# One pair of PSUM banks for two spreadings, and quarter loads of the last down group's weights into staging tiles

## The chip, the cores and the metric

The kernel runs on one core of a Trainium2 chip. The metric is the device time of one execution in microseconds (us). Engines are called PE (TensorE matmul), PEld (its weight loads), DVE (VectorE), ACT (ScalarE), POOL (GpSimd) and SP (SyncE, which issues nearly all DMAs here).

## The reference

One layer of a streaming encoder, for 1024 prompt tokens and 64 sample tokens together (T = 1088 columns), model width 1024, all in float32: a mixer (retention and sliding-window attention), cross attention, and a SwiGLU feed-forward, each with a residual add, then a final RMS norm. The change touches the feed-forward and what leads into it:

```python
def rms_norm(x, g=None):
    y = xf * lax.rsqrt(jnp.mean(xf * xf, axis=-1, keepdims=True) + EPS)
    ...
def swiglu(x, g_ffn, w_gate, w_up, w_down):
    hn = rms_norm(x, g_ffn)
    return (jax.nn.silu(hn @ w_gate) * (hn @ w_up)) @ w_down
...
hp = hp + swiglu(hp, g_ffn[l], w_gate[l], w_up[l], w_down[l])
y_prompt = rms_norm(hp, g_final)
```

D_FF is 2816, that is 22 blocks of 128 rows.

## The kernel before, in words

Activations lie transposed: 128 partitions of features, 1088 columns of tokens, split into two halves of 544 columns, each worked in two pieces of 272. Every float32 operand is split into a rounded high part (a cast on ACT, L123) and the rest (a subtraction on DVE, L124), and a product is three matmuls: high by high, high by low, low by high (L205, L206 and L208 in the feed-forward, L149 to L151 elsewhere).

**The products of the feed-forward** are Strassen's (Winograd's form): weights and operands are taken as 2 by 2 blocks, and seven products P1 to P7 replace eight. `strassen` (L247) runs them in the order P1 (operand B11), P2 (B21), P6 (T2), P5 (T1), P7 (T3), P3 (B22), P4 (T4); DVE and POOL add up the sums u1, u2, u5, u3. The weights' side is made by `weight_ops` (L166) from two raw tiles of two halves each (a11, a12; a21, a22): POOL forms a11-a21 for P7 (L183), a21+a22 for P5 (L184), a22-a11 for P6 (L186) and a12-that for P3 (L189), in place, and every result is cast and subtracted into a tile `wq`. So P6 comes after a chain: cast and subtraction of a11 (P1), L183, cast and subtraction (P7), L186, cast (P6).

**Spreading.** A norm factor per token is found with tokens on partitions (`some_rstd`) and is spread to all partitions by three 128x128 matmuls with the identity into a PSUM tile (`spread`, L323, matmuls L330) and a copy on ACT (L331). The 1088 columns go in chunks of 384, 384 and 320. After cross attention the first chunk is spread at once; the other two are put in `self.later` (L1263) and run inside the first, plain gate product (`plain`, L225): three of its four sums are open, each in a pair of banks, when `run_later` spreads chunk 1 and chunk 2. The PSUM pool has four pairs of banks ("pst", L1331). What follows them on PE is the fourth sum, beginning with operand B12 (tile `b12`).

**Down projection** (`down`, L1443). The 22 blocks are taken in groups of 8, 8 and 6. In each group the eight 128-row strips of the output go in four pairs, m = 0, 2, 4, 6, called here pair 1 to pair 4. The sums stay in tiles y: y[0] is `rstd_f`, the others show as y0, y1, y2. DVE adds a product to y (L1453), POOL adds a sum u (L1455). In the last group (n = 384 columns per block) P2 and P4 are left out of Strassen's seven and are computed by a tail (`finish`, products L149 with weights `wb`), so a pair has five products: P1, P6, P5, P7, P3. When the second half of a strip is complete, `complete` (L1459) squares it on ACT (L1463 for the first, L1466 into a tile `sq` for the others) and DVE adds the square to `rstd` (L1467). After pair 3 ACT loads the table for the square root and takes a dummy root (L1504).

The weights of a pair are loaded into two raw tiles (pool of two buffers), each 128x768 in the last group, by SP (L117). The operands of the next group are loaded back from memory (`fetch`, L1435) into **staging tiles** named `hl` and are then cast and subtracted into the operand tiles. The staging tiles rotate over two pools: "hl" with 4 buffers (L1330) and "hl2" with 6 (L1408), two tiles from "hl", then three from "hl2":

```python
self.pools = (self.hl, self.hl, more, more, more) * 2   # set once, L1409
self.pools = self.pools[1:] + self.pools[:1]            # per tile, in fetch
...
sq = self.hl.tile([P, HALF], F32, tag="hl", name="sq")  # complete
```

Which of the two a tile falls on is set by how many were taken before it. The `sq` tiles of `complete` come from pool "hl" too. In the last group B21 and T4 are fetched after pair 1's products are written down.

**What sets the order.** Each engine runs its own queue in order. A scheduler with a model of the times decides the order of the instructions on each engine when the kernel is built, SP's loads among them; a tile that takes over a buffer makes its first writer wait for the last user of the tile before it. So an edit can move instructions of lines that it doesn't touch.

Of the kernel before, what the change touches and what calls it, by code (L numbers as in the profile page):

```python
# [11 lines left out]
F32 = mybir.dt.float32  # L12
# [7 lines left out]
P = 128  # L20
# [20 lines left out]
HALF = T // 2  # L41
# [68 lines left out]
class Kernel:  # L110
# [54 lines left out]

    def weight_ops(self, raws, n=512, skip=()):  # L166

        nc = self.nc
        half = [[raws[i][:, j * n:(j + 1) * n] for j in range(2)] for i in range(2)]
        (a11, a12), (a21, a22) = half  # L170
        add, sub = ALU.add, ALU.subtract
        w = {}

        def put(name, src):
            if name in skip:
                return
            q = w[name] = self.new_op()
            self.split(src, q[:, 0, :n], q[:, 1, :n])

        tt = nc.gpsimd.tensor_tensor  # L180
        put("P1", a11)
        put("P2", a12)
        tt(out=a11, in0=a11, in1=a21, op=sub)  # L183
        tt(out=a21, in0=a21, in1=a22, op=add)  # L184
        put("P7", a11)
        tt(out=a11, in0=a22, in1=a11, op=sub)  # L186
        put("P6", a11)
        put("P5", a21)
        tt(out=a12, in0=a12, in1=a11, op=sub)  # L189
        put("P3", a12)  # L190
        put("P4", a22)
        return w
# [127 lines left out]

        return [(min(a, n - P), P) for a in range(0, n, P)]

    def spread(self, out, r):  # L323

        nc = self.nc
        n = out.shape[1]
        spans = self.spans(n)
        pb = self.norm_psum("pb")
        for i, (a, w) in enumerate(spans):
            nc.tensor.matmul(pb[:, a:a + w], r[:, i:i + 1].broadcast_to([P, P]), self.ident, start=True, stop=True)  # L330
        nc.scalar.copy(out, pb[:, :n])  # L331
# [898 lines left out]
    def cross_out_phase(self):  # L1230
        nc, tc, io = self.nc, self.tc, self.io
        with ExitStack() as ctx:
            cq = ctx.enter_context(tc.tile_pool(name="cq", bufs=1, reuse_waits="tile"))
            ctx.enter_context(self.plain_psum(side="right"))
            pn = ctx.enter_context(tc.tile_pool(name="pnc", bufs=1, reuse_waits="tile", space=PSUM, side="right"))
            self.norm_psum = lambda name: pn.tile([P, 512], F32, tag="n", name=name)
            xg = self.ring_tiles(0, KT // 2, "xg", F32)
            self.xg = [xg[k // 2][:, k % 2, :] for k in range(KT)]
            self.ops, self.slots = {}, {}
            units = [lambda m=m: self.unit(io["w_co"][m], KT) for m in range(KT)]  # L1240
            norms, rs = [], []
            for m, u, (c0, n) in self.m_major(units, CH, tail=2):
                if m == 4 and not self.ops:
                    self.operands_early()
                    self.first_sums()
                x = cq.tile([P, 384], F32, tag="hx", bufs=4, name="hx")[:, :n]
                self.load(x, self.d_h[0][m, :, c0:c0 + n])
                ps = self.dense(u, self.couts, c0, n)
                nc.vector.tensor_tensor(out=x, in0=ps, in1=x, op=ALU.add)
                self.store(self.d_h[1][m, :, c0:c0 + n], x)  # L1250
                acc = self.rstd_f[:, c0:c0 + n]
                nc.vector.scalar_tensor_tensor(self.xg[m][:, c0:c0 + n], x, self.gains[:, 2, m:m + 1],
                                               self.rstd[:, c0:c0 + n], ALU.mult, ALU.mult)
                self.add_square(acc, x, m == 0, cq, n)
                if m == KT - 1:
                    root = self.root[:, c0 // 384, :]
                    def first(acc=acc, root=root):
                        rs.append(self.some_rstd(acc, times=root))

                    norms.append((first, lambda acc=acc, i=len(norms): self.spread(acc, rs[i])))  # L1260
                    if len(norms) < 3:
                        self.later += norms[-1][:3 - len(norms)]
            self.later, self.last_roots = [norms[1][1], norms[2][1]], norms[2][0]  # L1263

    def op_tiles(self, ring, names):
        for a in range(0, len(names), 2):
# [168 lines left out]
    def fetch(self, name, group):  # L1435
        n0 = sum(GROUPS[:group]) // 2
        for k in range(GROUPS[group] // 2):
            self.pools = self.pools[1:] + self.pools[:1]
            a = self.pools[0].tile([P, HALF], F32, tag="hl", name="hl")
            self.load(a, self.d_op[OPS.index(name), n0 + k])  # L1440
            yield a

    def down(self, starts):  # L1443
        nc, io = self.nc, self.io
# [4 lines left out]
        half = lambda m, t: y[m][:, t * HALF:(t + 1) * HALF]  # L1449
        def add(m, i, t, ps, sb):  # L1450
            v = half(m + i, t).rearrange("p (b c) -> p b c", b=2)
            if ps is not None:
                nc.vector.tensor_tensor(out=v, in0=ps, in1=v, op=ALU.add)  # L1453
            if sb is not None:
                nc.gpsimd.tensor_tensor(out=v, in0=sb, in1=v, op=ALU.add)  # L1455
# [3 lines left out]
        def complete(m, c0, n):  # L1459
            acc, o = self.rstd[:, c0:c0 + n], y[m][:, c0:c0 + n]  # L1460
            if c0 not in begun:
                begun.add(c0)
                nc.scalar.activation(acc, o, AF.Square)  # L1463
            else:
                sq = self.hl.tile([P, HALF], F32, tag="hl", name="sq")[:, :n]
                nc.scalar.activation(sq, o, AF.Square)  # L1466
                nc.vector.tensor_tensor(out=acc, in0=acc, in1=sq, op=ALU.add)  # L1467

        def load_half(tile, m, a, b):
            self.load(tile.rearrange("p (k m) -> p k m", m=P), io["w_down"][m, :, a:b, :])  # L1470

        for gi, g in enumerate(GROUPS):
            last = gi == len(GROUPS) - 1
            f0, n = starts[gi], g * P // 2
            for m in range(0, KT, 2):
                def emit(i, t, ps, sb, m=m):
                    add(m, i, t, ps, sb)
                    if last and t == 1:
                        complete(m + i, HALF, HALF)

                raws = [self.wp.tile([P, 1024], F32, tag="raw", bufs=2, name="raw") for i in range(2)]
                for i in range(2):
                    load_half(raws[i][:, :2 * n], m + i, f0, f0 + g)
                if m == KT - 4 and not last:
                    for name in ("B11", "B21" if gi == 0 else "T2"):
                        self.ahead[name, gi + 1] = list(self.fetch(name, gi + 1))
                if gi == 0:
                    for i in range(2):
                        self.load(y[m + i], self.d_h[1][m + i])
                if m == 0 and not last:  # L1490
                    self.plain(self.plain_weights(raws, n), self.ops, emit)
                    for name in ("T2", "T1", "T3", "T4"):
                        self.load_operand(name, gi)
                else:
                    w = self.weight_ops(raws, n, ("P2", "P4") if last else ())
                    if m == KT - 2 and not last:
                        self.refill = lambda name, gi=gi: self.turn(name, 1) if gi == 0 else self.turn_last(name)
                    self.strassen(w, self.ops, emit, last)
                    self.refill = None
                    if m == 0:  # L1500
                        for name in ("B21", "T4"):
                            self.load_operand(name, gi)
                if last and m == KT - 4:
                    nc.scalar.activation(self.root[:, 0, :1], self.rstd[:, HALF:HALF + 1], AF.Sqrt)  # L1504
        rest = []
        for m in range(0, KT, 2):
            raw = self.wp.tile([P, 1024], F32, tag="raw", bufs=2, name="raw")
# [189 lines left out]
```

## Time and profile before

| | |
|---|---|
| three runs | 2239.42, 2241.54, 2242.42 us (median 2241.54) |
| profiled execution | 2239.58 us, span 2237.8 us from first to last instruction |
| mean granted PE clock | 0.986 |
| last down group, pair 1's first matmul | 2141.53 us |
| tail's first matmul | 2194.96 us |
| DMA over the span | 290.86 MB, mean 130 GB/s |

Times in the rows are us from the start of the span, then the duration. In a row of the timeline the square brackets give the idle time of the engine before it and what ended it. A row of stretches gives the busy time of each engine, with the count of its instructions, then PE's granted clock (1.00 is full), the DMA share and GB/s. At full clock matmuls with 272 columns follow each other every 0.125 us, while a row shows some 0.29 us for one, as they overlap. The tail of the span, from about 2219 us on, is a chain of norm steps and stores that neither part of the change touches.

### The profile page before, as it was taken

The numbers are of one execution on the slowest core, as the hardware profiler recorded it, in microseconds if no ns is written. First come the engines' busy times: TensorE is split into PE (matmuls) and PEld (weight loads), VectorE is DVE, ScalarE is ACT, GpSimd is POOL, SyncE is SP. The second block draws the span as 40 slices with busy tenths as digits, with TensorE's granted clock in tenths as the row PEclk, the third lists the DMA queues.
The fourth block names the chain that finished last, engine by engine and source line by source line (L and its number), as shares of the span: only waits on it lengthen the run. The fifth ranks groups of instructions, "written<-read, shape, count | busy, mean of one in ns | idle before, by whom it ended". The sixth has DMA issues, their size and how long they took to land.

```text
span 2237.8 us, 41757 instructions
## 1 busy us (share of the span) xinstructions
PE 2171.3 (97%) x16434; PEld 2106.8 (94%) x16434; DVE 1600.4 (72%) x2655; ACT 884.7 (40%) x1897; POOL 690.5 (31%) x466
## 2 busy tenths in 40 slices
PE   9999999999999989999999999999999999999996
PEld 9899999999999977779999998999999999999986
DVE  8986878676687668876455555668777777778588
ACT  7333333435444355553133333333222222334243
POOL 1441533342253112220000000014555555434462
PEclk9999999999999999999999999999999999999998
DMA  5433345443445475326443112422332332475233
GB/s 205 156 111 110 117 123 137 133 127 113 167 152 178 151 229 169 114 75 208 130 154 107 55 48 65 134 85 88 122 130 101 102 122 89 142 273 182 84 102 109
DMA packets 182599, 290.86 MB, mean 130 GB/s; under 512 B 40290, under 2 KB 110850, under 8 KB 182402
## 3 DMA queue, kind: packets, MB, share of 16 engines
q1 hardware_dynamic: 177794, 279.26, 39.3%
q10 hardware_dynamic: 4608, 8.91, 1.1%
q8 instruction: 130, 2.13, 0.4%
q14 instruction: 67, 0.55, 0.1%
HBM read 196.95 MB, written 91.16 MB: 129 GB/s over the span
## 4 chain that ended last, share of the span: by engine, by line
PE 75%; DVE 7%; DMA 4%; issue 1%; ACT 1%; POOL 1%; SPq 0%; DVEq 0%; ACTq 0%; POOLq 0%
PE pq L208 14%; PE pq L206 14%; PE pq L205 14%; PE pd L149 7%; PE pd L151 7%; PE pd L150 7%; PE pout L1000 1%; DMA hl<-d_op 1%; PE pp L984 1%; DVE wq L124 1%; PE pss L942 1%; DMA ld<-d_swa 1%; DVE B L124 1%; DMA raw<-w_ret_out 1%; PE pk L699 0%
## 5 line engine op out<-in xcount | busy, mean ns | idle before, releaser
L124 DVE TENSOR_TENSOR wq<-raw,wq 128x512 fp32r<-128x512 f32 (+1 forms) x505 | 450.1, 895 | 124.8 <-ACT wq L123 122.6
L123 ACT CAST wq<-raw 128x512 fp32r<-128x512 f32 (+1 forms) x505 | 307.6, 614 | 569.9 <-PE pq L208 262.7
L205 PE MATMUL pq<-T,wq 128*128 128x272 f32 x1832 | 493.9, 289 | 6.2 <-DVE u L252 3.6
L206 PE MATMUL pq<-T,wq 128*128 128x272 f32 x1832 | 493.9, 289 | 0.0
L206 PE MATMUL pq<-B,wq 128*128 128x272 f32 x1592 | 429.3, 289 | 8.4 <-DVE B L124 8.4
L205 PE MATMUL pq<-B,wq 128*128 128x272 f32 x1592 | 426.7, 288 | 0.0
L208 PE MATMUL pq<-T,wq 128*128 128x272 f32 x1832 | 384.4, 290 | 3.4 <-DVE wq L124 3.4
L183 POOL TENSOR_TENSOR raw<-raw 128x512 f32<-128x512 f32 (+1 forms) x59 | 79.4, 1345 | 894.8 <-DVE rs_r L291 483.8
L205 PEld LDWEIGHTS pq<-T,wq 128*128 128x128 f32 x1832 | 346.7, 189 | 7.1 <-DVE u L252 3.7
L206 PEld LDWEIGHTS pq<-T,wq 128*128 128x128 f32 x1832 | 346.8, 189 | 0.3 <-issue 0.3
L208 PE MATMUL pq<-B,wq 128*128 128x272 f32 x1592 | 334.0, 290 | 0.0
L206 PEld LDWEIGHTS pq<-B,wq 128*128 128x128 f32 x1592 | 300.7, 189 | 10.3 <-DVE B L124 10.0
L205 PEld LDWEIGHTS pq<-B,wq 128*128 128x128 f32 x1592 | 300.1, 189 | 0.7 <-issue 0.4
L208 PEld LDWEIGHTS pq<-T,wq 128*128 128x128 f32 x1832 | 292.0, 191 | 4.6 <-DVE wq L124 3.8
L208 PEld LDWEIGHTS pq<-B,wq 128*128 128x128 f32 x1592 | 253.5, 190 | 0.5 <-issue 0.3
L252 DVE TENSOR_TENSOR u<-pq,u 128x544 f32<-128x544 f32 x177 | 127.5, 720 | 111.7 <-PE pq L208 111.1
L186 POOL TENSOR_TENSOR raw<-raw 128x512 f32<-128x512 f32 (+1 forms) x59 | 85.3, 1446 | 125.2 <-DVE wq L124 122.6
L970 POOL TENSOR_TENSOR t<-t,den 128x768 f32<-128x768 f32 (+2 forms) x34 | 47.8, 1406 | 167.7 <-DVE den L968 49.9
L571 DVE TENSOR_TENSOR stage<-pq,u 128x544 f32<-128x544 f32 x112 | 80.3, 717 | 26.6 <-PE pq L208 25.8
L184 POOL TENSOR_TENSOR raw<-raw 128x512 f32<-128x512 f32 (+1 forms) x59 | 89.2, 1512 | 3.7
L1455 POOL TENSOR_TENSOR y<-u,y 128x544 f32<-128x544 f32 x38 | 62.6, 1658 | 72.4 <-DVE y L1453 54.4
L189 POOL TENSOR_TENSOR raw<-raw 128x512 f32<-128x512 f32 (+1 forms) x59 | 83.2, 1411 | 4.4
(373 smaller groups left out, 4674.2 us busy)
## 6 DMA issues: line engine op xcount, KB each, us to landing
hl<-d_op SPq DMA_DIRECT2D x85, 272.0 KB, 4.4
d_qkv<-stage SPq DMA_DIRECT2D x44, 272.0 KB, 2.3
d_op<-stage SPq DMA_DIRECT2D x44, 272.0 KB, 2.1
d_op<-ht SPq DMA_DIRECT2D x44, 272.0 KB, 3.3
raw<-w_gate SPq DMA_DIRECT2D x22, 512.0 KB, 3.5
raw<-w_up SPq DMA_DIRECT2D x22, 512.0 KB, 3.6
d_gate<-stage ACTq DMA_DIRECT2D x32, 272.0 KB, 2.8
raw<-w_down SPq DMA_DIRECT2D x16, 512.0 KB, 4.4
```

The costliest lines, as they stand in the source:

```text
L123: self.last_cast = self.nc.scalar.copy(hi, src).ins
L124: return self.nc.vector.tensor_tensor(out=lo, in0=src, in1=hi.bitcast(F32), op=ALU.subtract).ins
L149: mm(ps, wh, xh, start=start, stop=False)
L150: mm(ps, wh, xl, start=False, stop=False)
L151: self.last_mm = mm(ps, wl, xh, start=False, stop=stop).ins
L184: tt(out=a21, in0=a21, in1=a22, op=add)
L186: tt(out=a11, in0=a22, in1=a11, op=sub)
L189: tt(out=a12, in0=a12, in1=a11, op=sub)
L205: mm(ps[:, c, :HC], w[:, 0, ks], x[:, 0, cs], start=start, stop=False)
L206: mm(ps[:, c, :HC], w[:, 0, ks], x[:, 1, cs], start=False, stop=False)
L208: self.last_mm = mm(ps[:, c, :HC], w[:, 1, ks], x[:, 0, c * HC:(c + 1) * HC], start=False, stop=stop).ins
L252: add = lambda out, a, b: nc.vector.tensor_tensor(out=out, in0=a, in1=b, op=ALU.add)
```

## The change

Two things. The two later spreadings (chunks 1 and 2) write into the two banks of one pair instead of taking a pair each. And in the last down group, for pairs 2 to 4, the weights are no longer loaded into two raw tiles of 128x768 but as four quarters of 128x384, each into a staging tile of its own. The arithmetic is the same.

```diff
@@ weight_ops
+        quarters = [[raws[i][:, j * n:(j + 1) * n] for j in range(2)] for i in range(2)]
+        return self.quarter_ops(quarters, n, skip)
+
+    def quarter_ops(self, quarters, n=512, skip=()):
         nc = self.nc
-        half = [[raws[i][:, j * n:(j + 1) * n] for j in range(2)] for i in range(2)]
-        (a11, a12), (a21, a22) = half
+        (a11, a12), (a21, a22) = quarters
@@ spread
-    def spread(self, out, r):
+    def spread(self, out, r, pb=None):
...
-        pb = self.norm_psum("pb")
+        if pb is None:
+            pb = self.norm_psum("pb")
@@ cross_out_phase
+                    accs.append(acc)
...
-            self.later, self.last_roots = [norms[1][1], norms[2][1]], norms[2][0]
+
+            def spread_both():
+                banks = self.bank_pair()
+                for i in (1, 2):
+                    self.spread(accs[i], rs[i], banks[:, i - 1])
+
+            self.later, self.last_roots = [spread_both], norms[2][0]
@@ fetch
-            self.pools = self.pools[1:] + self.pools[:1]
-            a = self.pools[0].tile([P, HALF], F32, tag="hl", name="hl")
+            a = self.staging()
...
+    def staging(self):
+        self.pools = self.pools[1:] + self.pools[:1]
+        return self.pools[0].tile([P, HALF], F32, tag="hl", name="hl")
@@ down
-                raws = [self.wp.tile([P, 1024], F32, tag="raw", bufs=2, name="raw") for i in range(2)]
-                for i in range(2):
-                    load_half(raws[i][:, :2 * n], m + i, f0, f0 + g)
+                if last and m:
+                    quarters = [[self.staging()[:, :n] for j in range(2)] for i in range(2)]
+                    for i in range(2):
+                        for j in range(2):
+                            load_half(quarters[i][j], m + i, f0 + j * g // 2, f0 + (j + 1) * g // 2)
+                else:
+                    raws = [self.wp.tile([P, 1024], F32, tag="raw", bufs=2, name="raw") for i in range(2)]
+                    for i in range(2):
+                        load_half(raws[i][:, :2 * n], m + i, f0, f0 + g)
...
-                    w = self.weight_ops(raws, n, ("P2", "P4") if last else ())
+                    skip = ("P2", "P4") if last else ()
+                    w = self.quarter_ops(quarters, n, skip) if last and m else self.weight_ops(raws, n, skip)
```

In the order of the changed program's instructions L330, L331, L1453, L1455, L1466, L1467 and L1504 stand as L334, L335, L1467, L1469, L1480, L1481 and L1525, and L183, L186, L189 as L186, L189, L192.

More of the change, by code (lines that the diff above doesn't have):

```diff
@@ L1240, in cross_out_phase @@
             units = [lambda m=m: self.unit(io["w_co"][m], KT) for m in range(KT)]
-            norms, rs = [], []
+            norms, rs, accs = [], [], []
             for m, u, (c0, n) in self.m_major(units, CH, tail=2):
```

## The prediction

> **What bounds the kernel now.** I read the page first, then the stretches of 20 us at the end, then TensorE's timeline for its gaps.
>
> ```profile
> PE 2171.3 (97%) x16434; PEld 2106.8 (94%) x16434; DVE 1600.4 (72%) x2655; ACT 884.7 (40%) x1897; POOL 690.5 (31%) x466
> ...
> PE 75%; DVE 7%; DMA 4%; issue 1%; ACT 1%; POOL 1%; SPq 0%; DVEq 0%; ACTq 0%; POOLq 0%
> ```
>
> PE is busy 97% of 2237.8 us and carries 75% of the chain that ended last. So an edit counts by what it adds to or takes from PE's gaps. It touches two places: one spot near 1512 us, and the last down group, from pair 2 (m=2) on.
>
> ```profile
> 2140.00:2160.00 20.00, 19.04 (x151) 18.60 (x150) 18.18 (x21) 5.27 (x11) 13.91 (x10) 1.00 0.19 50
> 2160.00:2180.00 20.00, 15.62 (x106) 15.00 (x105) 14.96 (x19) 7.85 (x15) 14.41 (x11) 0.83 0.36 117
> 2180.00:2200.00 20.00, 18.63 (x149) 18.34 (x147) 16.06 (x20) 8.61 (x13) 12.80 (x10) 1.00 0.26 81
> ```
>
> Columns: length, then busy time of PE, PEld, DVE, ACT, POOL, then PE's granted clock. PE has room in the last group, above all at 2160 to 2180, where the clock is low too. Its gaps, and the rows that give the length of a product:
>
> ```profile
> 2152.73 0.29 PE L205 MATMUL pq<-B,wq 128*128 128x272 f32 x1
> 2155.91 0.39 PE L205 MATMUL pq<-T,wq 128*128 128x272 f32 x1 [0.78 <-ACT wq L123]
> 2169.30 0.39 PE L205 MATMUL pq<-T,wq 128*128 128x272 f32 x1 [1.17 <-DVE B L124]
> 2173.25 0.82 PE L208 MATMUL pq<-T,wq 128*128 128x272 f32 x2 [3.19 <-DVE wq L124]
> 2181.52 0.29 PE L205 MATMUL pq<-B,wq 128*128 128x272 f32 x1
> 2183.76 0.29 PE L205 MATMUL pq<-B,wq 128*128 128x272 f32 x1
> 2194.96 0.29 PE L149 MATMUL pq<-B,wb 128*128 128x272 f32 x1
> 2198.76 0.36 PE L149 MATMUL pq<-B,wb 128*128 128x272 f32 x1 [1.37 <-DVE y L1453]
> 2200.91 0.39 PE L149 MATMUL pq<-T,wb 128*128 128x272 f32 x1 [0.79 <-DVE y L1453]
> ```
>
> 2181.52 is the start of pair 3's P3 (B22), 2183.76 that of pair 4's P1 (B11): a product of 18 matmuls takes 2.24 us. 2152.73 is the start of pair 2's P1, 2194.96 the first product of the tail. Between lie 15 products, 33.6 us of work in 42.2 us: **8.6 us are lost there now**, and 1.37 + 0.79 = 2.2 more in the tail. That is all this edit can win in the last group.
>
> **Part 1, the shared pair of banks.** The rows:
>
> ```profile
> 1514.06 0.93 PE L330 MATMUL pb<-ident,rs_r 128*128 128x128 f32 x6 [2.05 <-ACT rstd_f L331]
> 1515.51 0.60 PE L205 MATMUL pq<-b,wq 128*128 128x272 f32 x1 [0.52 <-ACT rstd_f L331]
> 1514.37 0.65 ACT L123 CAST T<-xg 128x544 fp32r<-128x544 f32 x1 [0.36 <-DVE xg L1288]
> 1515.03 0.42 ACT L331 COPY rstd_f<-pb 128x320 f32<-128x320 f32 x1
> ```
>
> The 2.05 us look like the prize: the second spreading waits for the first one's copy because it takes the same buffer. But in the order of the changed program's instructions, with the waits of each, the second spreading still carries its wait for ACT:
>
> ```
> 9396 L334 Matmult pq_17084<-ident_63,rs_r_16773 128x128 [waits DVE_49]
> 9398 L334 Matmult pq_17084<-ident_63,rs_r_16960 128x128 [waits DVE_49,Activation_49]
> ```
>
> And without it nothing would come: PE's next product waits for ACT's second copy (the 0.52), and that copy stands in ACT's queue behind a cast that DVE releases and that ends at 1515.02. PE would resume at 1515.5 either way. I count **0** for this part; the ends are 0 and 0.5 us (the 0.52, if the pair freed another bank sooner).
>
> **Part 2, quarters in the staging tiles.** The work is the same: 20 casts, 20 subtractions, 16 POOL sums. The loads of pairs 2 to 4 become 12 of 192 KB instead of 6 of 384 KB, so SP issues 6 more; SP has idle time there and PE waits for none of those issues as such. What changes is where each wait lies. The program's order shows these:
>
> (a) Staging tiles rotate over one pool of 4 buffers ("hl") and one of 6 ("hl2"), two in five on "hl". The squares of the completed sums (L1466) also live in "hl". Pair 2's first quarter a11 gets the buffer of the square of pair 1's rstd_f, so its load waits for the last step of pair 1's last sum:
>
> ```
> 942 L117 DMACopy hl_24612<-w_down 128x384 [waits DMAHW5_49,DVE_49]
> 946 L117 DMACopy hl_24327<-w_down 128x384 [waits DMAHW1_49,DVE_49]
> ```
>
> The DVE wait of 946 is met by the addition of that square (L1467 of before). All five products of pair 2 stand behind a11. Now its weights are cast during pair 1, as soon as they land:
>
> ```profile
> 2145.58 0.51 ACT L123 CAST wq<-raw 128x384 fp32r<-128x384 f32 x1 [3.60 <-DMA raw<-w_down]
> ```
>
> (b) The scheduler, which expected the loads late, put casts and POOL sums behind other work. On ACT pair 3's first cast stands behind the squares of pair 2. On POOL pair 2's sums stand behind pair 1's last addition, where now they stand ahead of it. On ACT pair 4's cast for P7 stands behind two casts of the tail's weights, two squares, the table load and the root (L1504), and P6 needs what follows it.
>
> The durations:
>
> ```profile
> 2150.13 1.61 POOL L1455 TENSOR_TENSOR y<-u,y 128x544 f32<-128x544 f32 x1 [1.93 <-DVE y L1453]
> 2151.70 1.01 POOL L183 TENSOR_TENSOR raw<-raw 128x384 f32<-128x384 f32 x1
> 2160.78 1.36 POOL L1455 TENSOR_TENSOR rstd_f<-u,rstd_f 128x544 f32<-128x544 f32 x1 [1.13 <-DVE rstd_f L1453]
> 2163.04 0.51 ACT L123 CAST wq<-raw 128x384 fp32r<-128x384 f32 x1 [2.19 <-DMA raw<-w_down]
> 2163.46 0.66 ACT L1466 ACTIVATE sq<-rstd_f 128x544 f32<-128x544 f32 x1
> 2163.58 0.56 DVE L124 TENSOR_TENSOR wq<-raw,wq 128x384 fp32r<-128x384 f32 x1 [2.88 <-ACT wq L123]
> 2164.14 0.72 DVE L1467 TENSOR_TENSOR rstd<-rstd,sq 128x544 f32<-128x544 f32 x1
> raw<-w_down SPq DMA_DIRECT2D x8, 192.0 KB, 2.5
> ```
>
> *Pair 2.* Pair 1 ends at 2152.73 as now; nothing ahead of it moves. POOL then owes three additions. The first needs u3, which DVE can write (0.7) when POOL has ended the addition begun at 2150.13, so at 2152.3; three at 1.36 end at 2156.4. Then square 0.66, addition 0.72, load 2.5, cast 0.51, and 0.2 for five hand-overs: P1 starts at 2161.0. **PE waits 8.3 us** (0 now). From P1 to P6 there is a chain through DVE 0.56, POOL L183, two casts, DVE, POOL L186: from L183's start to P6's first matmul now 2155.91 - 2151.70 = 4.2, with the DVE step and hand-over 4.9. P1 covers 2.24 of it, so **2.65 more**. Pair 2: 10.9.
>
> *Pair 3.* Three additions of pair 2 begin 0.75 after its P7 and end 0.75 + 4.1 - 2.24 = 2.6 after its P3; with square, cast and hand-overs P1 starts 3.9 late. Then again P1 to P6, with an L1467 ahead on DVE: 4.9 + 0.2 - 2.24 = 2.9. Pair 3: 6.8.
>
> *Pair 4.* P1 is ready; P6 is not. These rows join in:
>
> ```profile
> 2156.35 3.30 POOL L1455 TENSOR_TENSOR y<-u,y 128x544 f32<-128x544 f32 x2
> 2158.36 1.71 DVE L124 TENSOR_TENSOR wq<-raw,wq 128x384 fp32r<-128x384 f32 x1
> 2190.68 0.84 ACT L123 CAST wb<-raw 128x768 fp32r<-128x768 f32 x1 [0.67 <-DMA raw<-w_down]
> 2193.35 1.28 ACT L1504 ACT_TABLE_LOAD   x1
> ```
>
> Lower end: ACT alone. Its first tail cast waits until P1 has read the slot (1.7 after P3), then two casts (0.75 apart), two squares and a u1 copy (some 0.56 apart), table load, root: 6.3. Then cast 0.51, DVE 0.56, POOL 1.0, cast 0.51, hand-overs 0.2: P6 at 9.1, less P1's 2.24: 6.9. Upper end: DVE and POOL in turn. The row at 2158.36 takes 1.71 where 0.56 is usual, and ends just after POOL's pair of additions (2159.65). Ahead of the root stand four such DVE steps (two of 0.87, two of 0.64) and three POOL steps (1.36, 1.0, 1.0) after an addition that ends at 2.9: 2.9 + 3.0 + 3.4 = 9.3, then 0.3 + 2.8: P6 at 12.4, less 2.24: 10.2. I take **10.2**, since that row shows them taking turns.
>
> *The clock after these waits.*
>
> ```profile
> 2170.00:2173.00 3.00, 0.07 (x1) 0.00 (x0) 3.00 (x4) 0.51 (x1) 1.70 (x3) 0.62 0.00 0
> 2173.00:2175.00 2.00, 1.75 (x7) 1.75 (x8) 2.00 (x3) 0.57 (x2) 1.39 (x1) 0.50 0.00 0
> 2175.00:2178.00 3.00, 3.00 (x16) 3.00 (x16) 1.55 (x3) 0.59 (x2) 2.01 (x2) 0.58 0.65 212
> ```
>
> After gaps of 1.17 and 3.19 us the granted clock was 0.5, and stayed so until about 2177.5, 4.2 us into the work: 2.1 us lost. Pair 2's slow P1 is covered by the POOL chain. I take 1.7 for pair 3 and 2.0 for pair 4, with 0 and 2.1 as ends for each.
>
> The Trainium skill, "TensorE: Matmul & The Clock Gate", section "What's actually happening", says that the clock halves after a wholly idle window of some 3.4 us and comes back after a busy one. By that rule pair 3, whose gaps are 3.9 and 2.9, need not lose its 1.7, and the sum would be 1.7 less. The trace differs: at 2170 the clock fell before any gap had lasted 3.4 us, so I keep the term.
>
> **The sum.** Added: 10.9 + 6.8 + 10.2 + 1.7 + 2.0 = 31.6. Gone: the 8.6 lost there now, and the tail's 2.2, since its weights are now cast earlier and DVE is not behind. Net **+20.8 us**. The profiled execution took 2239.58 us (span 2237.8): 2260.4. It lies 2.0 under the median 2241.54; the runs shown lie at 2239.42 to 2242.42. I say **2260**.
>
> **Rivals.**
> *A, faster.* The mechanism is prefetch: the staging tiles, 10 buffers instead of 2 raws, let weights land a pair ahead. It decides if a11's load is let go before pair 1's P3 ends at 2152.7 less some 8 us, that is, if its buffer's last reader is an operand cast and not the square. For it: 11 of the 12 quarters have no square as their last reader, and pair 4's a11 is cast long ahead. Against it: the wait of 946. Price: up to 8.6 + 2.2 = 10.8 gained: 2229.
> *B, half.* The late loads cost as worked out, but pair 4's chain is hidden (root early, DVE and POOL beside each other: 6.9), the clock stays up, and POOL runs ahead by one addition in pairs 2 and 3 (1.36 each): 20.8 - 3.3 - 3.7 - 2.7 = +11: 2251.
> *C, no change.* Part 1 does not do what it says, as worked out; part 2 would come to nothing if other products filled the new waits. PE's order in pairs 2 to 4 does take T1 and T3 between the halves of T2, but all of these come after P1, so they fill little: 2241.
>
> **Chances.** Forecast (2252 to 2267) 0.80; B (2246 to 2252) 0.10; above 2267 0.03; C 0.03; A 0.04. The range 2250 to 2267 takes in both ends of pair 4's chain (3.3) and of the clock terms. A measurement of this kernel can tell 0.2%, some 4.5 us, from no change. So faster 0.04, same 0.03, slower 0.93.
>
> **What would show it.** In the changed profile: PE idle some 8 us before the first matmul of pair 2, released by ACT's cast, ahead of it DMA hl<-w_down, ahead of that the addition of the square; about 4 us before pair 3; about 10 us before pair 4's P6, behind ACT's table load and root; granted clock 0.5 after them; the spreading's wait of about 2 us near 1514 still there. I am wrong if the load of a11 is issued before 2150, or if the last group ends no later than now.

## The result, and the profile after

| | before | after |
|---|---|---|
| median of six runs | 2242.24 us (2239.42 to 2244.98) | 2260.27 us (2256.97 to 2263.3) |
| profiled execution | 2239.58 us, span 2237.8 | 2262.3 us, span 2260.5 |
| first matmul of pair 1 | 2141.53 us | 2146.44 us |
| first matmul of the tail | 2194.96 us | 2220.93 us |

The changed kernel takes 1.0081 times as long, with a 95% interval of 1.0069 to 1.0093: 18.0 us more by the medians. The two profiled executions differ by 22.7 us, but 4.9 of that was there before pair 1 began, as the start of pair 1 shows. From there to the end are 96.27 us before and 114.06 after: **17.8 us more**. So I compare two lengths from here on: the *group* (from pair 1's first matmul to the tail's first) and the *tail* (from there to the end of the span). The group grew from 53.43 to 74.49 us, and the tail shrank from 42.84 to 39.57.

Line numbers below are those of the changed program; beside the ones listed above, L205, L206 and L208 stand there as L208, L209 and L211, and L252 and L255 as L255 and L258. The stretches of the end, after (same columns as in the prediction):

```profile
2140.00:2160.00 20.00, 17.80 (x144) 17.58 (x142) 18.26 (x24) 6.85 (x14) 10.53 (x8) 1.00 0.62 183
2160.00:2180.00 20.00, 13.88 (x90) 13.34 (x90) 10.20 (x14) 5.59 (x11) 8.39 (x8) 0.74 0.14 41
2180.00:2200.00 20.00, 15.80 (x108) 15.05 (x108) 10.66 (x14) 5.20 (x10) 11.30 (x10) 0.91 0.08 21
2200.00:2220.00 20.00, 10.80 (x65) 10.80 (x66) 11.15 (x12) 7.37 (x13) 6.98 (x6) 0.74 0.12 39
2220.00:2240.00 20.00, 20.00 (x164) 20.00 (x163) 16.84 (x42) 7.18 (x18) 4.74 (x3) 1.00 0.11 43
```

The totals hardly tell the kernels apart (PE is busy 2174.9 us, 2171.3 before): the work is the same. The stretches do: PE is idle for 6, 4 and 9 of 20 us in the last group, and then runs full in the tail. PE's timeline, after, with pair 1's P3, the gaps, pair 3's P3 and the tail's first product:

```profile
2155.40 0.29 PE L208 MATMUL pq<-B,wq 128*128 128x272 f32 x1
2165.47 0.60 PE L208 MATMUL pq<-B,wq 128*128 128x272 f32 x1 [7.68 <-ACT wq L123]
2170.29 0.55 PE L208 MATMUL pq<-T,wq 128*128 128x272 f32 x1 [0.36 <-ACT wq L123]
2183.41 0.39 PE L208 MATMUL pq<-B,wq 128*128 128x272 f32 x1 [3.69 <-ACT wq L123]
2188.45 0.40 PE L208 MATMUL pq<-T,wq 128*128 128x272 f32 x1 [0.72 <-ACT wq L123]
2195.36 0.29 PE L208 MATMUL pq<-B,wq 128*128 128x272 f32 x1
2209.20 0.60 PE L208 MATMUL pq<-T,wq 128*128 128x272 f32 x1 [9.20 <-ACT wq L123]
2220.93 0.29 PE L149 MATMUL pq<-B,wb 128*128 128x272 f32 x1
```

Each wait ends with ACT's cast. Read the rows as starts of products: 2155.40 is pair 1's P3; 2165.47 and 2170.29 are pair 2's P1 and P6, 2183.41 and 2188.45 pair 3's, 2195.36 is pair 3's P3 and 2209.20 pair 4's P6. What released pair 2's P1, by the timelines of POOL, ACT, DVE and SP (the SP row takes six loads together, of which the first is meant):

```profile
2159.70 1.33 POOL L1469 TENSOR_TENSOR rstd_f<-u,rstd_f 128x544 f32<-128x544 f32 x1
```
```profile
2161.06 0.66 ACT L1480 ACTIVATE sq<-rstd_f 128x544 f32<-128x544 f32 x1 [0.63 <-POOL rstd_f L1469]
...
2164.91 0.51 ACT L123 CAST wq<-hl 128x384 fp32r<-128x384 f32 x1 [1.56 <-DMA hl<-w_down]
```
```profile
2161.75 0.73 DVE L1481 TENSOR_TENSOR rstd<-rstd,sq 128x544 f32<-128x544 f32 x1 [3.19 <-ACT sq L1480]
```
```profile
2162.51 29.30 SPq L117 DMA_DIRECT2D hl<-w_down  x6
```

Sum, square, addition of the square, load, cast: one after the other, 2159.70 to 2165.47. The load of pair 2's a11, the first of the six, is issued at 2162.51, when the square's buffer is let go. It is the only one of the six that waited for a square.

Pair 3's wait is of another kind. ACT's timeline ahead of its P1:

```profile
2182.29 0.66 ACT L1480 ACTIVATE sq<-y 128x544 f32<-128x544 f32 x1 [0.63 <-POOL y L1469]
2182.86 0.50 ACT L123 CAST wq<-hl 128x384 fp32r<-128x384 f32 x1
```

No load is late here: the DMA engines moved nothing from 2175.2 us up to this cast, so its weights had landed more than 7 us ahead. The cast stands in ACT's queue behind pair 2's squares, which wait for POOL's sums; that is the order the scheduler chose.

### The profile page after: what moved, and what is told of

The parts are those of the page before. It is cut to its first block, busy times and chain, and to the rows that moved or that the text cites. A ratio compares the mean times of both kernels' runs of the same rounds, so it can differ in the third digit from the quotient of the medians.

```text
span 2260.5 us, 41771 instructions
## 1 busy us (share of the span) xinstructions
PE 2174.9 (96%) x16434; PEld 2111.0 (93%) x16434; DVE 1599.3 (71%) x2655; ACT 884.4 (39%) x1897; POOL 688.8 (30%) x466
## 5 line engine op out<-in xcount | busy, mean ns | idle before, releaser
L123 ACT CAST wq<-raw 128x512 fp32r<-128x512 f32 (+1 forms) x490 | 300.3, 617 | 547.5 <-PE pq L211 260.5
L124 DVE TENSOR_TENSOR wq<-raw,wq 128x512 fp32r<-128x512 f32 (+1 forms) x490 | 432.2, 885 | 114.7 <-ACT wq L123 112.2
L208 PE MATMUL pq<-T,wq 128*128 128x272 f32 x1832 | 494.4, 289 | 14.9 <-ACT wq L123 10.3
L209 PE MATMUL pq<-T,wq 128*128 128x272 f32 x1832 | 494.0, 289 | 0.0
L208 PE MATMUL pq<-B,wq 128*128 128x272 f32 x1592 | 428.3, 289 | 11.5 <-ACT wq L123 11.4
L209 PE MATMUL pq<-B,wq 128*128 128x272 f32 x1592 | 430.0, 290 | 8.1 <-DVE B L124 8.1
L211 PE MATMUL pq<-T,wq 128*128 128x272 f32 x1832 | 383.2, 290 | 0.0
L208 PEld LDWEIGHTS pq<-T,wq 128*128 128x128 f32 x1832 | 347.3, 190 | 16.4 <-ACT wq L123 11.1
L186 POOL TENSOR_TENSOR raw<-raw 128x512 f32<-128x512 f32 (+1 forms) x56 | 76.2, 1361 | 895.1 <-DVE rs_r L294 485.7
L209 PEld LDWEIGHTS pq<-T,wq 128*128 128x128 f32 x1832 | 347.1, 189 | 0.3 <-issue 0.3
L211 PE MATMUL pq<-B,wq 128*128 128x272 f32 x1592 | 335.0, 290 | 0.1
L208 PEld LDWEIGHTS pq<-B,wq 128*128 128x128 f32 x1592 | 301.1, 190 | 12.7 <-ACT wq L123 11.8
L209 PEld LDWEIGHTS pq<-B,wq 128*128 128x128 f32 x1592 | 301.2, 189 | 10.1 <-DVE B L124 9.7
L211 PEld LDWEIGHTS pq<-T,wq 128*128 128x128 f32 x1832 | 291.5, 191 | 0.8 <-issue 0.8
L211 PEld LDWEIGHTS pq<-B,wq 128*128 128x128 f32 x1592 | 254.3, 191 | 0.8 <-issue 0.3
L255 DVE TENSOR_TENSOR u<-pq,u 128x544 f32<-128x544 f32 x177 | 127.4, 720 | 124.4 <-PE pq L211 123.9
L189 POOL TENSOR_TENSOR raw<-raw 128x512 f32<-128x512 f32 (+1 forms) x56 | 82.3, 1469 | 127.3 <-DVE wq L124 124.7
L1469 POOL TENSOR_TENSOR y<-u,y 128x544 f32<-128x544 f32 x38 | 60.1, 1591 | 86.7 <-DVE y L1467 51.4
L187 POOL TENSOR_TENSOR raw<-raw 128x512 f32<-128x512 f32 (+1 forms) x56 | 85.2, 1521 | 3.5
L192 POOL TENSOR_TENSOR raw<-raw 128x512 f32<-128x512 f32 (+1 forms) x56 | 79.9, 1427 | 4.2
```

The lines of the kernel that those rows point to most:

```text
L123: self.last_cast = self.nc.scalar.copy(hi, src).ins
L124: return self.nc.vector.tensor_tensor(out=lo, in0=src, in1=hi.bitcast(F32), op=ALU.subtract).ins
L208: mm(ps[:, c, :HC], w[:, 0, ks], x[:, 0, cs], start=start, stop=False)
L209: mm(ps[:, c, :HC], w[:, 0, ks], x[:, 1, cs], start=False, stop=False)
L211: self.last_mm = mm(ps[:, c, :HC], w[:, 1, ks], x[:, 0, c * HC:(c + 1) * HC], start=False, stop=stop).ins
L255: add = lambda out, a, b: nc.vector.tensor_tensor(out=out, in0=a, in1=b, op=ALU.add)
```

## The experiments

The medians are of 5 to 12 executions. The ratio is to the kernel before on the same chip; group and tail are those of the profiled execution. The diffs are cut to the lines that matter; `hl2` in them stands for the pool of that name. The theory at the start: the loads are held back by the squares' buffers, and the casts and sums behind them. The rivals: the quarters as such, the scheduler's order whatever the buffer, part 1.

| run | median us | ratio (95%) | group | tail |
|---|---|---|---|---|
| before | 2242.24 | | 53.43 | 42.84 |
| after | 2260.27 | 1.0081 (1.0069 to 1.0093) | 74.49 | 39.57 |
| e1_banks_only | 2242.14 | 1.0001 (0.9989 to 1.0012) | 52.79 | 42.66 |
| e7_hl2_only | 2242.44 | 1.0001 (0.9992 to 1.0011) | 51.12 | 45.49 |
| e8_one_on_hl | 2243.23 | 1.0012 (1.0003 to 1.0021) | 56.06 | 44.03 |
| e9_one_off_hl | 2252.73 | 1.0054 (1.0041 to 1.0066) | 69.54 | 39.47 |
| e6_root_late | 2260.67 | 1.0079 (1.0067 to 1.0091) | 75.59 | 39.57 |
| e10_drawn_early | 2241.13 | 0.9995 (0.9986 to 1.0004) | 54.40 | 43.04 |
| e11_ops_at_4 | 2248.97 | 1.0029 (1.0020 to 1.0038) | 52.72 | 46.01 |
| e12_tail_strips | 2239.83 | 0.9992 (0.9984 to 1.0000) | 51.47 | 43.80 |
| e13_sums_on_dve | 2235.39 | 0.9969 (0.9957 to 0.9980) | 46.73 | 44.73 |
| e14_no_squares | 2235.95 | 0.9972 (0.9961 to 0.9983) | 49.93 | 39.88 |
| e15_raws_tail_strips | 2244.23 | 1.0010 (0.9998 to 1.0021) | 53.86 | 43.69 |
| e16_before_sums_dve | 2237.39 | 0.9977 (0.9968 to 0.9986) | 49.91 | 41.45 |

**Which part costs the time.** Part 1 alone (the last group back to raw tiles):

```diff
-                if last and m:
+                if last and m > 99:
```

> Part 1 alone: the two spreadings share a pair of banks, the last down group loads raw tiles as before. My theory: 0, at most 0.5 us either way beyond what the phase of the clock's windows gives (up to 1.7 us, half a window of 3.41 us, at the low clock after that wait). The second spreading still waits about 2.05 us for ACT's copy and the next product 0.5 us. Rival (the pair frees a bank, the wait of 2.05 us goes): 2 us faster. Rival (part 1 is behind some of the 18 us): several us slower.

No difference, and the waits at the spreadings are there after as they were before. PE's timeline of the changed kernel:

```profile
1518.58 1.55 PE L334 MATMUL pq<-ident,rs_r 128*128 128x128 f32 x6 [2.04 <-ACT rstd_f L335]
1520.64 0.60 PE L208 MATMUL pq<-b,wq 128*128 128x272 f32 x1 [0.52 <-ACT rstd_f L335]
```

2.04 and 0.52 us, where before had 2.05 and 0.52. All of the 18 us is part 2's.

**Quarters, or the buffers they get?** The changed kernel with all quarters from "hl2", where no square lives:

```diff
-quarters = [[self.staging()[:, :n] for j in range(2)] for i in range(2)]
+quarters = [[hl2.tile([P, HALF], F32, tag="hl", name="hl")[:, :n] for j in range(2)] for i in range(2)]
```

> The changed kernel, but all twelve quarters come from the pool of 6 buffers that holds no square. Loads are as many and as small as in the changed kernel. My theory (the squares' buffers hold back the loads, and the casts behind them): no wait before pair 2's and pair 3's P1, pair 4's P6 not behind the root, so the group loses none of the 29.7 us it loses in the changed kernel, and also none of the 8.6 that it lost before, nor the tail's waits: 2230 us, 12 below the kernel before; up to 2234 if a few waits stay. Rival (the quarters themselves, as six more and smaller loads, cost the time): 2255 to 2260. Rival (the scheduler's placing of the sums and casts costs it, whatever the buffer): 2245 to 2255.

The 18 us are gone, with as many and as small loads. So the quarters themselves cost nothing that can be told, the shared buffer does, and with it goes the order that the scheduler built on it: here pair 3's first cast is done by 2161.1, 17 us ahead of pair 2's first square (2178.34). But 2230 was wrong: the kernel gained nothing on the one before. PE's timeline of this run shows where the rest went:

```profile
2172.24 0.39 PE L208 MATMUL pq<-T,wq 128*128 128x272 f32 x1 [0.69 <-DVE B L124]
2174.20 0.72 PE L211 MATMUL pq<-T,wq 128*128 128x272 f32 x2 [1.20 <-DVE wq L124]
2197.11 0.39 PE L149 MATMUL pq<-B,wb 128*128 128x272 f32 x1 [0.59 <-DVE u L255]
2202.62 0.56 PE L149 MATMUL pq<-B,wb 128*128 128x272 f32 x1 [2.85 <-DVE y L1467]
```

The long waits before P1 and P6 are gone; what ends the ones that are left is DVE each time. The group is 2.3 us shorter than before, the tail 2.65 longer. The first theory (the loads are the bound, take their waits away and 12 us are won) falls for this part; the new one, still to be tested, is that **DVE's queue bounds the last group**, and whatever is not waited for in the pairs is waited for in the tail.

Two runs put one buffer the other way. e8 is e7 with pair 2's a11 alone on "hl"; e9 is the changed kernel with pair 2's a11 alone on "hl2":

```diff
 e8: (hl if (m, i, j) == (2, 0, 0) else hl2).tile(...)
 e9: + if m == 2: quarters[0][0] = hl2.tile(...)[:, :n]
```

> As the run with all quarters in the pool without squares, but for one: pair 2's a11 is drawn from the pool of 4, and gets the buffer of pair 1's square. My theory: pair 2 alone pays its 7.8 us before P1 and 2.6 before P6, pairs 3 and 4 run through: about 10.4 above the run without squares, so 2241. Rival (one load among twelve can be caught up by the products of later pairs): within 3 us of the run without squares. Rival (a late pair 2 makes the later pairs late too): 2255 to 2260.

> The changed kernel, but pair 2's a11 is drawn from the pool of 6; pair 3's and pair 4's quarters lie as before. My theory: pair 2's 7.8 + 2.6 us go, pair 3's 3.9 + 2.8 and pair 4's 9.4 + 2.8 (clock) stay: 2260 - 10.4 = 2250. Rival (it all hangs on pair 2's lateness, which the schedule then carries on): near 2232. Rival (pair 2's lateness is covered by something else): 2258 to 2262.

e8, PE's timeline:

```profile
2159.17 0.60 PE L208 MATMUL pq<-B,wq 128*128 128x272 f32 x1 [7.89 <-ACT wq L123]
2163.96 0.59 PE L208 MATMUL pq<-T,wq 128*128 128x272 f32 x1 [0.35 <-ACT wq L123]
```

One load in one buffer brings back pair 2's wait as it was (7.89 where the changed kernel had 7.68), and no other: pairs 3 and 4 run through. Yet by the medians that costs 0.8 us over e7, not 10.4. While PE waits, DVE works off its queue: in the profiled executions the group pays 4.9 over e7 and the tail gets 1.5 back. Between 0.8 and those 3.5 these runs don't decide. 2241 was near the mark, but by two misses that cancel. e9, PE's timeline:

```profile
2172.64 0.60 PE L208 MATMUL pq<-B,wq 128*128 128x272 f32 x1 [7.38 <-ACT wq L123]
...
2200.01 0.59 PE L208 MATMUL pq<-T,wq 128*128 128x272 f32 x1 [9.20 <-ACT wq L123]
```

Pair 2 no longer waits, so pair 3 waits twice as long (7.38 for 3.69): its cast (2172.10) still stands behind pair 2's squares, and POOL, which adds the sums for these, first idles 4.46 us for DVE. Pairs 3 and 4 keep their waits, as expected, but of the 10.4 us only 7.5 come back. The waits of the pairs are not independent terms.

**Pool, or order of drawing?** e10 keeps both pools, but draws and loads a pair's quarters ahead of the products of the pair before, so ahead of its squares:

```diff
+                    if last and m < KT - 2:
+                        ahead = [[self.staging()[:, :n] for j in range(2)] for i in range(2)]
+                        for i in range(2):
+                            for j in range(2):
+                                load_half(ahead[i][j], m + 2 + i, f0 + j * g // 2, f0 + (j + 1) * g // 2)
                     self.strassen(w, self.ops, emit, last)
```

> The changed kernel with both pools, but each pair's four quarters are drawn from the pools and loaded before the products of the pair ahead, so ahead of that pair's squares in the rotation. My theory (it is the order of drawing that puts a load behind a square, not the pool as such): no wait of 3 us or more before a P1, the group within 3 us of the run with all quarters in the pool without squares: 2240 to 2246. Rival (the pool of 4 is too small for squares and quarters whatever the order): 2250 or more.

No wait before a P1 is over 1.0 us, and the time is as expected: the order of drawing decides, not the pool as such. Its group is 3.3 us longer than e7's, a little more than I gave it. One long wait is left, before pair 3's P6 (PE's timeline):

```profile
2173.95 0.39 PE L208 MATMUL pq<-T,wq 128*128 128x272 f32 x1 [4.62 <-ACT wq L123]
```

That cast follows POOL's L189, which stands behind two of POOL's additions; no load is part of it.

**Pair 4's chain.** The rows of the changed kernel, ACT, DVE, POOL:

```profile
2202.48 1.28 ACT L1525 ACT_TABLE_LOAD   x1
2206.34 0.20 ACT L1525 ACTIVATE root<-rstd 128x1 f32<-128x1 f32 x1 [2.57 <-DVE rstd L1481]
```
```profile
2203.12 1.75 DVE L124 TENSOR_TENSOR wb<-raw,wb 128x768 fp32r<-128x768 f32 x1
2204.79 1.52 DVE L1481 TENSOR_TENSOR rstd<-rstd,sq 128x544 f32<-128x544 f32 x1
2206.98 0.56 DVE L124 TENSOR_TENSOR wq<-hl,wq 128x384 fp32r<-128x384 f32 x1 [0.67 <-ACT wq L123]
```
```profile
2202.57 1.48 POOL L186 TENSOR_TENSOR hl<-hl 128x384 f32<-128x384 f32 x1
2204.13 1.59 POOL L187 TENSOR_TENSOR hl<-hl 128x384 f32<-128x384 f32 x1
```

ACT idles 2.57 us for DVE's addition of the second square, and DVE and POOL stretch each other: 1.75 and 1.52 us on DVE (0.72 for the latter in the prediction's row), 1.48 and 1.59 on POOL where 1.01 is usual. e6 takes the root out of the chain:

```diff
-                if last and m == KT - 4:
+                if last and m == KT - 2:
                     nc.scalar.activation(self.root[:, 0, :1], ...)
```

> The changed kernel with the dummy root and its table load (L1525) moved from behind pair 3 to behind pair 4 in the program; ACT's cast for pair 4's P7 then follows the second square at once. My theory (DVE and POOL in turn set the root's time, so the cast is ready early but its subtraction still stands on DVE behind the additions of both squares, which end at 2206.3 in the changed kernel's trace, where the subtraction now starts at 2207.0): pair 4's wait of 9.2 us shortens by 0.7 only, 2259.6 in all. Rival (table load and root on ACT are the bound): the wait shortens by 2.4, up to 3.8 with the clock, 2256 to 2258. Rival (the table load now falls into the tail and is paid there): 1.3 us slower, 2261.5.

PE's timeline and DVE's:

```profile
2207.68 0.59 PE L208 MATMUL pq<-T,wq 128*128 128x272 f32 x1 [8.46 <-ACT wq L123]
```
```profile
2204.03 1.52 DVE L1481 TENSOR_TENSOR rstd<-rstd,sq 128x544 f32<-128x544 f32 x1
2205.47 0.55 DVE L124 TENSOR_TENSOR wq<-hl,wq 128x384 fp32r<-128x384 f32 x1
```

The wait fell from 9.20 to 8.46, by 0.74, and the subtraction stands right behind the square on DVE. Table load and root were not the bound. In the total that is too little to be seen.

**Is it DVE?** Four runs from e7. e11 moves the preparation of B21 and T4 from behind pair 1 (`if m == 0`) to behind pair 3 (`if m == 4`). e12 loads the tail's weights in strips into "hl2":

```diff
 e12:
-            raw = self.wp.tile([P, 1024], F32, tag="raw", bufs=2, name="raw")
+            for i in range(2):
+                raw = hl2.tile([P, HALF], F32, tag="hl", name="hl")[:, :n]
...
+                self.last_queued = self.split(raw, q[:, 0, i * n:(i + 1) * n], q[:, 1, i * n:(i + 1) * n])
```

> As the run with all quarters in the pool without squares, but B21 and T4, which only the tail reads, are fetched, cast and subtracted behind pair 3 instead of behind pair 1. In that run PE lost 0.69 and 1.20 us in pair 3 behind these subtractions on DVE, and 1.7 us by the clock after it; then 2.85 us in the tail, and 3.4 by the clock. My theory (DVE and POOL, not the weights, bound the last group, and what is not waited for in the pairs is waited for in the tail): pair 3's 3.6 us go, the tail loses as much more: 2240 to 2244, no different. Rival (these subtractions stand in the way and the tail has room): 2237 to 2239.

> As the run with all quarters in the pool without squares, and the tail's weights too are loaded strip by strip into that pool of 6 instead of two raw tiles; its casts and subtractions become 8 of 384 columns instead of 4 of 768. In that run DVE stood 1.07 us for the third and fourth raw load, with the additions that free PE's banks behind it: 2.85 us in the tail, 3.4 by the clock. My theory: no load is waited for, the tail's wait falls to about 1.5 us, too short for the clock to fall: 4 to 5 us less, 2238. Rival (DVE has too much queued in front of those additions, loads or not, and 8 subtractions take longer than 4): the wait stays at 2.5 us or more, 2242 to 2245.

e11 missed: 2249, 6.5 us over e7. It is no clean test, for the edit also moved work of the second down group, as PE's timeline of e11 shows:

```profile
2063.72 0.59 PE L209 MATMUL pq<-B,wq 128*128 128x272 f32 x1 [5.04 <-DVE B L124]
```

e7 has waits of 0.69, 0.77 and 1.34 us there. What is left to the last group and the tail is 1.6 and 0.5 us more than in e7: nothing gained by moving DVE's work later, as the theory has it. e12 came to 2239.8, at the edge of what can be told from the kernel before, short of the 2238 that I gave it; its tail's longest wait ahead of the norm fell to 1.38 us:

```profile
2198.27 0.38 PE L149 MATMUL pq<-B,wb 128*128 128x272 f32 x1 [1.38 <-DVE y L1467]
```

e15, raw tiles for the pairs and strips for the tail, stays at 2244, against my guess: if e12's small gain is real, it takes the quarters and the strips together.

> The pairs' weights in raw tiles as in the kernel before, only the tail's weights strip by strip in the pool of 6. It tells what the tail strips alone bring. My theory (the 0.1 per cent between the run with quarters and tail strips and the kernel before comes from the tail, whose raw loads waited): 2239 to 2241. Rival (it needs the pairs' quarters out of the raw tiles as well): 2242 to 2245.

Then DVE's load itself. e14 is e12 without seven of the eight squares and their additions on DVE. e13 is e12 with the 16 additions of the last group's sums on DVE instead of POOL:

```diff
 e13 (the flag is set where the groups begin):
-                nc.gpsimd.tensor_tensor(out=v, in0=sb, in1=v, op=ALU.add)
+                (nc.vector if self.last_group else nc.gpsimd).tensor_tensor(out=v, in0=sb, in1=v, op=ALU.add)
```

> As the run with quarters and tail strips in the pool without squares, but seven of the eight squares of the completed second halves (ACT) and their additions to rstd (DVE) are left out, so the norm of those columns counts one strip of eight. My theory (DVE's queue bounds the last group and the tail): 7 steps of some 0.75 to 1.5 us less on DVE, 4 to 6 us faster, 2234 to 2236. Rival (PE waits for weights or for POOL, not for DVE's load): within 1 us, 2239 to 2241.

> As the run with quarters and tail strips in the pool without squares, and in the last group the 16 additions of the sums u to y go from POOL to DVE: 16 of some 0.71 us more on DVE, 16 of 1.36 to 1.9 us fewer on POOL. My theory (DVE and POOL take turns where both work, so a POOL addition of 1.36 stretches DVE's steps by nearly as much): DVE's subtractions of 0.9 to 2.0 us return to 0.56, which pays for the 11.4 us added; within 4 us of that run, 2236 to 2244. Rival (POOL works beside DVE at no cost): DVE is late by most of the 11.4 us, 2247 to 2251.

e14: 3.9 us less for seven small steps, as a bound on DVE would have it (ACT lost seven squares too; the run doesn't separate them). e13 gives DVE *more* instructions and has the lowest median of all: **2235.4**, 0.9969 of the kernel before, 0.6 under my range. DVE's groups of instructions between the first matmul of pair 1 and the tail (count, then busy us and mean ns), e12 and then e13:

```profile
L124 DVE TENSOR_TENSOR wq<-hl,wq 128x384 fp32r<-128x384 f32 x15 | 16.2, 1098 | 3.5 <-ACT wq L123 3.5
L255 DVE TENSOR_TENSOR u<-pq,u 128x544 f32<-128x544 f32 x10 | 7.1, 712 | 0.1
```
```profile
L124 DVE TENSOR_TENSOR wq<-hl,wq 128x384 fp32r<-128x384 f32 x15 | 9.9, 677 | 1.7 <-ACT wq L123 1.7
L1469 DVE TENSOR_TENSOR y<-u,y 128x544 f32<-128x544 f32 x11 | 8.5, 788 | 0.0
L255 DVE TENSOR_TENSOR u<-pq,u 128x544 f32<-128x544 f32 x10 | 7.1, 713 | 0.1
```

The same 15 subtractions take 16.2 us beside 16 of POOL's additions and 9.9 beside the 3 that are left there; that alone pays for most of the 8.5 added. The last run makes this edit to the kernel before and nothing else:

> The kernel before, raw tiles and all, with one edit: in the last group the 16 additions of the sums u to y go from POOL to DVE. My theory (in the kernel before, the two waits of 1.17 and 3.19 us in pair 3 and the 2.1 us by the clock after them come from DVE and POOL taking turns, not from the weights' buffers): these 6.5 us go, the tail's waits stay, 2235 to 2238. Rival (it needs the quarters in the pool without squares too, because raw tiles are let go late): 2240 to 2244.

2237.4, 0.9977 of the kernel before, with the raw tiles kept. The intervals of e13 and e16 overlap, so the quarters and strips in e13 add nothing that can be told. Its two waits of 1.17 and 3.19 us shrink to this (PE's timeline of e16):

```profile
2164.53 0.39 PE L205 MATMUL pq<-T,wq 128*128 128x272 f32 x1 [1.37 <-ACT wq L123]
2165.92 0.37 PE L205 MATMUL pq<-T,wq 128*128 128x272 f32 x1 [0.64 <-ACT wq L123]
...
2179.05 0.51 PE L208 MATMUL pq<-T,wq 128*128 128x272 f32 x2 [0.92 <-DVE wq L124]
```

I had 6.5 us going in the group and the tail as it was; the group gave 3.5 and the tail 1.4.

What stays open: POOL's sums of the weights also no longer stand behind its additions in e13 and e16, and no run separates that from the stretching. So the runs show that taking POOL's additions away shortens the last group (51.47 to 46.73 us from e12 to e13, 53.43 to 49.91 from the kernel before to e16); that DVE's queue alone is the bound is argued, not shown.

## Why the prediction was right

A product is 2.24 us, and from pair 1's P3 (2155.40) to the tail 16 products would take 35.8. So each term can be read off the starts of the products.

| step of the prediction | predicted | measured, after |
|---|---|---|
| part 1 | 0 | 0 (e1) |
| pair 2 waits for a11 | 8.3 | 2165.47 - 2155.40 - 2.24 = 7.8 |
| pair 2, P1 to P6 | 2.65 | 4.82 - 2.24 = 2.6 |
| pair 3 waits for its first cast | 3.9 | 2183.41 - 2170.29 - 8.96 = 4.2 |
| pair 3, P1 to P6 | 2.9 | 5.04 - 2.24 = 2.8 |
| pair 3, clock | 1.7 | 2195.36 - 2188.45 - 6.72 = 0.2 |
| pair 4's P6 | 10.2 | 2209.20 - 2195.36 - 4.48 = 9.4 |
| pair 4, clock | 2.0 | 2220.93 - 2209.20 - 8.96 = 2.8 |
| sum added | 31.6 | 29.7 |
| gone: lost now in the group | -8.6 | -8.6 |
| gone: the tail's waits | -2.2 | 39.57 - 42.84 = -3.3 |
| net | +20.8 | +17.8 |

- **Part 1** is nothing, and for the reason given: the second spreading waits for ACT in both orders.
- **Pair 2 and pair 3** came as worked out, link by link: for pair 2 the addition of the square lets the load go, for pair 3 the cast stands behind the squares on ACT. e7, where both waits are gone, shows that the shared buffers are behind both (for pair 3 by way of the order built on them), and e8 that one load is enough for pair 2's wait.
- **Pair 4.** 10.2 rested on DVE and POOL taking turns, against a lower end of 6.9 by ACT alone (rival B). 9.4 was measured, and e6 shows that ACT's table load and root are not the bound.
- **The clock** is the term mis-sized. Pair 3's 1.7 was paid nowhere, because the POOL chain covered the slow P1 there just as I had argued for pair 2. Pair 4's P6 has no such cover and paid 2.8, above the 2.1 that I gave as its end.
- **The tail** gave back 3.3, not 2.2.
- **The time.** 2260 us against a median of 2260.27 is nearer than the working deserves. The net was 3.0 us too large, and it was added to an execution 2.7 us under the median of before's six runs.
- **Rival A** would not have won its 10.8 even with its condition met: e7 meets it, and the kernel is where it was. "All this edit can win" was a bound; new waits, each released by DVE, took it all back.

## What to carry to other kernels

When a transfer gets a buffer from a rotating pool, ask who read that buffer last: a load can be held back by a step at the end of the chain that it is to feed, and moving it to a pool without that reader, or drawing it earlier, removed all 18 us here. Waits of successive stages are not a sum: when one goes, look for the queue behind it, here most likely DVE's, before counting a gain. And where two engines stretch each other, giving the busier engine the other one's work can make the kernel faster, as e16 shows.

## What the runs showed of the hardware

**DVE beside POOL.** In these two runs only DVE's steps with both inputs in SBUF are stretched. The subtractions (L124) averaged 1098 ns in e12 and 677 in e13, but the additions that read a PSUM bank (L255, u<-pq,u) 712 and 713. The Trainium skill, "SBUF — State Buffer", section "SBUF: two separate sides", states the rule: DVE with two SBUF inputs and a GpSimd operation that reads SBUF exclude each other for a whole instruction. The trace agrees.

**The granted clock goes in windows of 3.41 us.** In the changed kernel it changed at 2160.43, 2170.67, 2184.32, 2187.74, 2204.80 and 2215.04 us: 3, 4, 1, 5 and 3 times 3.41 apart. Stretches of that length (busy PE is the second number, the clock the third from the end):

```profile
2180.91:2184.32 3.41, 0.84 (x5) 0.63 (x5) 2.35 (x3) 1.72 (x3) 1.41 (x3) 1.00 0.00 0
2184.32:2187.74 3.42, 3.41 (x14) 3.09 (x14) 0.92 (x1) 0.51 (x1) 2.85 (x3) 0.50 0.00 0
2197.98:2201.39 3.41, 2.02 (x17) 1.80 (x15) 1.77 (x3) 2.10 (x4) 2.76 (x3) 1.00 0.00 0
2201.39:2204.80 3.41, 0.00 (x0) 0.00 (x0) 3.41 (x4) 2.36 (x3) 3.33 (x3) 1.00 0.35 115
...
2208.21:2211.63 3.42, 2.43 (x10) 2.43 (x11) 1.85 (x3) 1.44 (x3) 1.39 (x2) 0.50 0.00 0
2211.63:2215.04 3.41, 3.41 (x17) 3.41 (x16) 0.00 (x0) 0.00 (x0) 0.00 (x0) 0.50 0.00 0
```

In all of them the work of a window goes with the clock of the next. After 0.84 us of work the clock halved, after 2.02 it did not; after 2.43 at half clock it stayed, after 3.41 it came back (1.00 from 2215.04 on). In the kernel before, the window that ended at 2170.69 had the work of this row, and the clock fell to 0.50:

```profile
2167.28:2170.69 3.41, 1.62 (x11) 1.18 (x10) 3.41 (x5) 1.54 (x4) 2.37 (x2) 1.00 0.00 0
```

So 1.62 us of work in 3.41 was too little there. The Trainium skill, "TensorE: Matmul & The Clock Gate", section "What's actually happening", gives the length of the window, some 3.4 us, and that it runs free of the kernel's start; the trace agrees. It has the clock halve after an idle window; here the window needn't be idle. By its wording pair 3 need not have slowed: it did (0.84 us of work in the window), and only the POOL chain made that cost nothing. That the windows' place differs between executions shows at the spreading: the same six matmuls took 0.93 us before, where the clock halved at 1515.33, behind them, and 1.55 after, where it halved at 1518.72, within them.
